# Grouped-query attention on one core: the one-block ScalarE tile of three-block jobs moves into the second bank of the transposes' tile

## The chip, the cores and the metric

The kernel runs on one core of one Trainium2 chip. The metric is the device time of the program in microseconds (us). A core has engines that run side by side, each in the order of its own program: TensorE (PE; its weight loads are listed as PEld), VectorE (DVE), ScalarE (ACT), GpSimd (POOL) and SyncE (SP, which issues transfers). They wait for each other through semaphores. Matmul results go to PSUM, eight banks of 512 float32 values on each of 128 partitions; everything else lies in SBUF.

## The reference

Attention with 32 query heads and 8 key/value heads, 8 batches, 512 positions, head size 64, all float32:

```python
batch, seq, n_heads, n_kv_heads, dim = 8, 512, 32, 8, 64
...
scores = np.einsum('bhqd,bhkd->bhqk', Q, K_expanded) * scale
weights = np.exp(scores - np.max(scores, axis=-1, keepdims=True))
weights = weights / (np.sum(weights, axis=-1, keepdims=True) + 1e-10)

output = np.einsum('bhqk,bhkd->bhqd', weights, V_expanded)
```

`K_expanded` and `V_expanded` repeat each key/value head for its four query heads; `scale` is 1/8.

## The kernel before

**Jobs and blocks.** One job is one key/value head of one batch with its four query heads: 64 jobs, `j` = 0 to 63. The four query heads are two pairs (`i` = 0, 1), the 512 keys four chunks of 128 (`kc`), and `m` is the head within a pair. A block is the scores of one head for one chunk of keys: 128 keys on the partitions, 512 queries in the free dimension, one PSUM bank. A job has 16 blocks. For every block the exponential of the scores is written to `pt` in fp16; the maximum is not subtracted. A second path for inputs outside its bounds, `general_path`, follows at the end and does not run for these inputs.

**Who takes the exponential.** ScalarE takes most blocks, two at a time: `act_tile(j, n)` makes the scores of its blocks in a tile `ps` of two banks (L199) and reads them with one ACTIVATE (L217). VectorE and GpSimd take the first two or three blocks of pair 1, with integer arithmetic: VectorE makes `u` from the scores (L228) and `f` from `u` (L249), GpSimd makes `g` and `w` from `f` (L241, L245), and VectorE adds `u` and `w` into `pt` (L262, in `exp_d4`, one job later). Three blocks are taken in the wide jobs, `WIDE(j)`: j = 10, 12, ..., 62, which is 27 jobs. ScalarE has 14 blocks in seven tiles of two in the other jobs. In a wide job it has 13: tiles 0 to 3 are pair 0, tile 4 is one single block (pair 1, chunk 1, `m` = 1, which stands in the second half of its tile), and tiles 5 and 6 are two blocks each.

**PSUM.** All eight banks are taken: `s_pool` has two score tiles of two banks, used in turn by `act_tile`; `d_pool` has one tile of two banks, used in turn by VectorE's score blocks and by the transposes of Q; `pv_pool` has one tile of two banks for the output sums. A tile that is asked for again is only written when its last readers are done.

**Order.** The order of every engine's work is written out by hand, in the loop over the jobs. While job `j` makes its scores, the product of weights and values (`pv`, L293) of job `j - 1` is cut into pieces that stand between the score tiles: pair 0 in two halves of 16 matmuls ahead of tile 2 and tile 3, pair 1 in pieces cut at `cut`, behind tiles 4, 5 and 6. For wide jobs `cut` is (4, 18): 4, 14 and 14 matmuls. `norm` divides by the sums (L336, L340) and frees the `pv` tile. Within `pv(j, 1)` the chunks of keys are taken in the order 2, 3, 1, 0, so the blocks that VectorE writes come last.

**Around the change.** Behind tile 3 the loop asks for a `d_ps` tile, `bank`. Into its first half `trans_q` writes the eight transposes of the queries of job `j + 2` (L164), as bf16, 1024 columns wide, which fills one bank. VectorE copies them to `qt` (L167). Then come `exp_d4` of the job before (L262), `exp_d2` of this job (L249, which sets GpSimd going), and tile 4. In odd jobs the second half of `bank` takes the third VectorE block of the wide job that follows. In wide jobs from 10 to 60 the second half stays unused; job 62 has no transposes.

Of the kernel before, what the change touches and what calls it, by code (L numbers as in the profile page):

```python
# [11 lines left out]
FP32 = mybir.dt.float32  # L12
# [46 lines left out]
def fast_path(ctx, tc, Q, K, V, out, flag):  # L59
    nc = tc.nc  # L60
    B, S, H, D = Q.shape
# [22 lines left out]
    s_pool = ctx.enter_context(tc.tile_pool(name="sps", bufs=2, space=PS))  # L84
# [15 lines left out]
    def load_k(b, lo=0, hi=KV):  # L100
        if b not in kn:
            kn[b] = knat_pool.tile([128, SC, KV, D], BF16, name="k_nat")
        nc.gpsimd.dma_start(  # L103
            out=kn[b][:, :, lo:hi, :],
            in_=K[b, :, lo:hi, :].rearrange("(sc p) g d -> p sc g d", p=128),
        )


    def load_v(b, lo=0, hi=KV, chunks=range(SC)):
        for sc in chunks:  # L110
            nc.gpsimd.dma_start(  # L111
                out=vt[b % 2][:, sc, lo:hi, 0:D],
                in_=V[b, sc * 128:(sc + 1) * 128, lo:hi, :],
            )
# [6 lines left out]
    def load_q(u, cuts=(0, 2 * HPG)):  # L121
        b, gp = divmod(u, GP)
        h0 = gp * 2 * HPG
        qn[u] = qnat_pool.tile([128, SC, 2 * HPG, D], BF16, name="q_nat")
        for lo, hi in zip(cuts[:-1], cuts[1:]):
            nc.gpsimd.dma_start(  # L126
                out=qn[u][:, :, lo:hi, :],
                in_=Q[b, :, h0 + lo:h0 + hi, :].rearrange("(sc p) h d -> p sc h d", p=128),
            )

    def d_tile():
        return d_pool.tile([128, 2, S], FP32, name="d_ps")
# [15 lines left out]
    def dma_k(b):  # L148
        kt[b] = kt_pool.tile([128, 2, GP, S], BF16, name="kt")
        for sc in range(SC):  # L150
            nc.sync.dma_start_transpose(
                out=kt[b][:, 0, :, sc * 128:(sc + 1) * 128],
                in_=kn[b][:, sc, :, :].rearrange("p g d -> p (g d)"),
            )
        for to, of in ((0, 64), (64, 0)):
            nc.sync.dma_start(out=kt[b][to:to + 64, 1, :, :], in_=kt[b][of:of + 64, 0, :, :])

    def trans_q(j, bank, lo=0, hi=NPAIR):
        u, g = divmod(j, 2)
        ps = bank.bitcast(BF16).rearrange("p (i sc c) -> p i sc c", i=NPAIR, sc=SC)  # L160
        for i in range(lo, hi):
            for sc in range(SC):
                h = g * HPG + 2 * i
                nc.tensor.transpose(ps[:, i, sc, :], qn[u][:, sc, h:h + 2, :], ident)  # L164
        if u not in qt:
            qt[u] = qt_pool.tile([128, 2, NPAIR, S], BF16, name="qt")
        return lambda: nc.vector.tensor_copy(  # L167
            out=qt[u][:, g, lo:hi, :], in_=ps[:, lo:hi, :, :].rearrange("p i sc c -> p i (sc c)")
        )

    def check_v(b, sc):
        n = b * SC + sc
        nc.vector.tensor_reduce(  # L173
            out=okv[:, n:n + 1], in_=vt[b % 2][:, sc, :, 0:D], op=ALU.max, axis=AX.XY,
            apply_absolute_value=True,
        )
# [6 lines left out]
    def taken(j):  # L183
        return 3 if WIDE(j) else 2

    def act_tiles(j):
        every = [(i, kc, m) for i in range(NPAIR) for kc in range(SC) for m in range(2)]
        first = DPAIR * SC * 2
        mine = [n for n in range(len(every)) if not first <= n < first + taken(j)]
        groups = [[n for n in mine if n // 2 == h] for h in range(len(every) // 2)]  # L190
        return [[every[n] for n in group] for group in groups if group]
# [3 lines left out]
    def scores(j, ps, i, kc, m):  # L195
        u, g = divmod(j, 2)
        b, gp = divmod(u, GP)
        keys = kt_first[:, gp, :, :] if b == 0 else kt[b][:, :, gp, :]
        nc.tensor.matmul(  # L199
            ps,  # L200
            keys[64 * m:64 * m + 64, g ^ m, kc * 128:(kc + 1) * 128],
            qt[u][64 * m:64 * m + 64, g, i, :],
            start=True,
            stop=True,
        )

    def open_job(j):
        pt = pt_pool.tile([128, NPAIR, SC, 2, S], FP16, name="pt")
        jobs.setdefault(j, {}).update(pt=pt, pv={})

    def act_tile(j, n):
        group = act_tiles(j)[n]
        i, kc, lo = group[0]
        ps = s_pool.tile([128, 2, S], FP32, name="s_ps")
        for _, _, m in group:
            scores(j, ps[:, m, :], i, kc, m)
        nc.scalar.activation(  # L217
            out=jobs[j]["pt"][:, i, kc, lo:, :], in_=ps[:, lo:, :], func=EXP, scale=scale
        )

    def exp_d(j, lo, hi, ps):
        st = jobs.setdefault(j, {})
        if "u" not in st:
            for name, dtype in (("u", I16), ("f", I16), ("g", BF16), ("w", BF16)):
                st[name] = dve_pool.tile([128, 3, S], dtype, name=name + "16")[:, 0:taken(j), :]
        for n in range(lo, hi):
            scores(j, ps[:, n - lo, :], DPAIR, n // 2, n % 2)
        return lambda: nc.vector.tensor_scalar(  # L228
            out=st["u"][:, lo:hi, :], in0=ps[:, 0:hi - lo, :], scalar1=A_U, scalar2=B_U,
            op0=ALU.mult, op1=ALU.add,  # L230
        )


    def by_pool(j):
        return 3 <= j < NJOB - 1
# [19 lines left out]
    def exp_d3(j, engine):  # L255
        st = jobs[j]
        correction(engine, st["f"], st["g"], st["w"])
# [144 lines left out]
    bank = d_tile()  # L402
# [4 lines left out]
    bank = d_tile()  # L407
# [3 lines left out]
    for j in range(NJOB):  # L411
        end = j == NJOB - 1
        last = j - 1
        late = last >= 0
        u, g = divmod(j, 2)
        b, gp = divmod(u, GP)
        open_job(j)
        if j == 1:

            nc.gpsimd.tensor_copy(out=gate, in_=jobs[0]["pt"][0:1, 0, SC - 1, 0, 0:1])  # L420
            load_q(2)
            load_q(3)
        if g == 0 and u >= 1 and u + 3 < NU:
            load_q(u + 3)
        if (gp, g) == (1, 0) and b + 1 < B:
            load_k(b + 1)
        if 3 <= 2 * gp + g < 3 + SC and b + 1 < B:
            load_v(b + 1, chunks=(2 * gp + g - 3,))
        if gp == 2 and g == 0 and b + 1 < B:
            dma_k(b + 1)  # L430

        cut = (4, 18) if taken(j) > 2 else (11, 19)
        act_tile(j, 0)
        if j == 0:
            trans_q(0, bank[:, 1, :], 1, NPAIR)()
            act_tile(j, 1)
            exp_d(j, 0, 2, d_tile())()
        else:
            exp_d(j, 0, 2, d_tile())()
            act_tile(j, 1)  # L440

        if j == 8:
            check_v(0, 0)
        if g == (b < B - 1) and j > 1:
            check_v(b, gp)
        if late:
            pv(last, 0, 0, 16)
        act_tile(j, 2)
        if late:
            pv(last, 0, 16, 32)  # L450
            norm(last, 0)
        act_tile(j, 3)

        reads = []
        if not end:
            bank = d_tile()

            ahead = (j + 1,) if j < 7 else (8, 9) if j == 7 else (j + 2,)
            for n, to in enumerate(ahead):
                if to < NJOB:  # L460
                    reads.append(trans_q(to, bank[:, n, :]))
            if j == 1:
                for swap in range(2):
                    reads.append(first_k(1, swap, bank[:, 1, swap * S // 2:]))
            elif j > 1 and b == 0 and gp + 1 < GP:
                reads.append(first_k(gp + 1, g, bank[:, 1, :]))
        else:
            pv(j, 0, 0, 16)
        for read in reads:
            read()  # L470

        if late and by_pool(last):
            exp_d4(last)
        check_sums()
        exp_d2(j)
        if not by_pool(j):
            exp_d3(j, nc.vector)
            exp_d4(j)
        act_tile(j, 4)
        if late:  # L480
            pv(last, 1, 0, cut[0])
        act_tile(j, 5)
        if not end and taken(j + 1) > 2:
            exp_d(j + 1, 2, taken(j + 1), bank[:, 1:2, :])()
        if late:
            pv(last, 1, *cut)
        act_tile(j, 6)
        if late:
            pv(last, 1, cut[1], 32)
            norm(last, 1)  # L490
            del jobs[last]
        if end:
            pv(j, 0, 16, 32)
            norm(j, 0)
            pv(j, 1, 0, 32)
            norm(j, 1)
# [118 lines left out]
```

## Time and profile before

| | |
|---|---|
| median time of three runs | 424.62 us (lowest 424.06) |
| span of the profiled execution, first to last instruction | 422.0 us |
| granted TensorE clock, mean | 0.984 |
| busy, share of the span: TensorE / VectorE / ScalarE / GpSimd | 91% / 82% / 96% / 69% |
| one ACTIVATE of two blocks (421) / of one block (27) | 1086 / 753 ns |
| scores, one matmul of 512 columns | 372 to 388 ns |

The profiled execution has no time of its own beside its span; 424.62 us is the median of executions that were timed. Durations of ScalarE's instructions overlap: a new one starts before the last has ended, so the step from one end to the next is shorter than a duration. Idle time is put down to the engine that ended it. Matmul durations overlap as well, and the two scores of a tile run side by side.

### The profile page before, as it was taken

To read this page: it belongs to the slowest core of one execution; us is meant where nothing else is said; L and a number is where in the kernel's file an instruction comes from. 1 tells how busy PE (TensorE), PEld (TensorE's weight loads), DVE (VectorE), ACT (ScalarE), POOL (GpSimd) and SP (SyncE) were. 2 spreads that over 40 slices of the span, in tenths; PEclk is the share of its full clock that TensorE was granted. 3 is DMA by queue.
4 is the path that set the end of the run, shared out by engine and by line. 5 is a ranking of instruction groups with operands and counts; after the bars stand their busy time and mean duration, and the time that the engine had idled before them with its cause. 6 is when DMAs were issued, how large, how long until landed. Compare 5 with 4: busy or idle time off the path is not lost.

```text
span 422.0 us, 13063 instructions
## 1 busy us (share of the span) xinstructions
PE 385.7 (91%) x5689; PEld 233.6 (55%) x5689; DVE 344.9 (82%) x611; ACT 404.2 (96%) x449; POOL 291.8 (69%) x209
## 2 busy tenths in 40 slices
PE   6889999999999999999999999999999999999983
PEld 2446565555555555555555555555555555555552
DVE  2697788889888888888888888888989888898875
ACT  3899999999999999999999999999999999999992
POOL 8504656778758876787866887677885887666560
PEclk9599999999999999999999999999999999999998
DMA  9996986599967998499964999649996799642223
GB/s 97 177 139 159 217 165 151 70 207 187 191 151 99 216 198 160 133 198 133 229 150 116 206 163 255 157 69 200 157 225 155 122 206 207 148 123 101 102 91 115
DMA packets 91438, 66.95 MB, mean 159 GB/s; under 512 B 52080, under 2 KB 74608, under 8 KB 91376
## 3 DMA queue, kind: packets, MB, share of 16 engines
q0 software_dynamic: 56544, 25.17, 51.1%
q1 hardware_dynamic: 34832, 40.90, 34.5%
q8 instruction: 45, 0.74, 0.7%
q14 instruction: 17, 0.14, 0.1%
HBM read 50.33 MB, written 33.55 MB: 199 GB/s over the span
## 4 chain that ended last, share of the span: by engine, by line
ACT 54%; PE 36%; DVE 6%; issue 1%; POOL 1%; ACTq 0%; DVEq 0%; POOLq 0%
ACT pt L217 54%; PE s_ps L199 17%; PE pv L293 16%; PE d_ps L199 1%; DVE o_sb L340 1%; PE d_ps L164 1%; DVE pt L262 1%; DVE u L228 1%; DVE qt L167 1%; DVE w L245 0%; POOL q_nat L126 0%; DVE kt_first L146 0%; ACTq L217 0%; PE d_ps L143 0%; DVE f L249 0%
## 5 line engine op out<-in xcount | busy, mean ns | idle before, releaser
L217 ACT ACTIVATE pt<-s_ps 128x1024 f16<-128x1024 f32 (+1 forms) x448 | 402.9, 1066 | 9.1 <-PE s_ps L199 9.0
L293 PEld LDWEIGHTS <-pt 128*128 128x128 f16 x4096 | 144.2, 98 | 86.8 <-issue 50.4
L293 PE MATMUL pv<-v,pt 128*128 128x65 bf16 x4032 | 183.2, 195 | 2.6 <-DVE o_sb L340 1.6
L199 PE MATMUL s_ps<-qt,kt 64*128 64x512 bf16 x757 | 152.7, 384 | 19.9 <-ACT pt L217 15.4
L245 POOL TENSOR_TENSOR w<-g,f 128x1024 bf16<-128x1024 bf16 (+1 forms) x60 | 153.7, 2562 | 5.0
L241 POOL TENSOR_SCALAR g<-f 128x1024 bf16<-128x1024 int16 (+1 forms) x60 | 73.9, 1231 | 110.1 <-DVE f L249 110.1
L228 DVE TENSOR_SCALAR u<-d_ps 128x1024 int16<-128x1024 f32 (+1 forms) x91 | 96.2, 1058 | 1.1 <-PE d_ps L199 1.1
L340 DVE TENSOR_TENSOR o_sb<-pv,inv 128x512 f32<-128x512 f32 x125 | 86.5, 692 | 4.5 <-DVE inv L336 0.2
L199 PEld LDWEIGHTS <-kt 64*128 64x128 bf16 x896 | 49.0, 93 | 62.6 <-issue 35.0
L336 DVE RECIPROCAL inv<-pv 128x8 f32<-128x8 f32 x125 | 25.9, 207 | 55.8 <-PE pv L293 55.4
L262 DVE TENSOR_TENSOR pt<-u,w 128x1536 uint16<-128x1536 int16 (+1 forms) x64 | 50.9, 795 | 0.2
L167 DVE COPY qt<-d_ps 128x1024 bf16<-128x1024 bf16 (+1 forms) x65 | 44.3, 683 | 4.5 <-PE d_ps L164 2.9
L164 PE MATMUL d_ps<-ident,q_nat 128*128 128x128 bf16 x512 | 40.1, 222 | 1.1 <-DVE kt_first L146 0.9
L164 PEld LDWEIGHTS <-q_nat 128*128 128x128 bf16 x512 | 29.2, 98 | 15.8 <-issue 15.7
L199 PE MATMUL d_ps<-qt,kt 64*128 64x512 bf16 x139 | 31.4, 376 | 0.3
L249 DVE TENSOR_SCALAR f<-u 128x1536 int16<-128x1536 int16 (+1 forms) x64 | 30.8, 481 | 0.0
L111 POOL DMA_DIRECT2D v<-in_V_dram x32 | 29.0, 910 | 0.4 <-issue 0.4
L126 POOL DMA_DIRECT2D q_nat<-in_Q_dram x34 | 27.4, 806 | 1.5 <-DMA q_nat<-in_Q_dram 1.3
L199 PE MATMUL s_ps<-qt,kt_first 64*128 64x512 bf16 x112 | 23.7, 419 | 4.1 <-ACT pt L217 3.0
L173 DVE TENSOR_REDUCE okv<-v 128x1 f32<-128x512 bf16 x32 | 21.6, 675 | 0.0
L199 PEld LDWEIGHTS <-kt_first 64*128 64x128 bf16 x128 | 8.0, 95 | 12.2 <-issue 8.4
L103 POOL DMA_DIRECT2D k_nat<-in_K_dram x10 | 7.7, 770 | 1.0 <-POOLq L599 0.8
(40 smaller groups left out, 37.6 us busy)
## 6 DMA issues: line engine op xcount, KB each, us to landing
out_dram<-o_sb SPq DMA_DIRECT2D x31, 1024.0 KB, 6.9
q_nat<-in_Q_dram POOLq DMA_DIRECT2D x31, 512.0 KB, 6.3
k_nat<-in_K_dram POOLq DMA_DIRECT2D x7, 512.0 KB, 8.6
v<-in_V_dram POOLq DMA_DIRECT2D x28, 128.0 KB, 7.6
kt<-kt SPq DMA_DIRECT2D x14, 256.0 KB, 4.6
out_dram<-o_sb SPq DMA_DIRECT2D x4, 256.0 KB, 2.4
kt<-k_nat SPq DMA_TRANSPOSE x28, 5.6
v<-in_V_dram POOLq DMA_DIRECT2D x4, 96.0 KB, 7.8
```

Source lines behind the costliest of these rows:

```text
L111: nc.gpsimd.dma_start(out=vt[b % 2][:, sc, lo:hi, 0:D], in_=V[b, sc * 128:(sc + 1) * 128, lo:hi, :],)
L164: nc.tensor.transpose(ps[:, i, sc, :], qn[u][:, sc, h:h + 2, :], ident)
L167: return lambda: nc.vector.tensor_copy(out=qt[u][:, g, lo:hi, :], in_=ps[:, lo:hi, :, :].rearrange("p i sc c -> p i (sc c)"))
L199: nc.tensor.matmul(ps, keys[64 * m:64 * m + 64, g ^ m, kc * 128:(kc + 1) * 128], qt[u][64 * m:64 * m + 64, g, i, :], start=True, stop=True,)
L217: nc.scalar.activation(out=jobs[j]["pt"][:, i, kc, lo:, :], in_=ps[:, lo:, :], func=EXP, scale=scale)
L228: return lambda: nc.vector.tensor_scalar(out=st["u"][:, lo:hi, :], in0=ps[:, 0:hi - lo, :], scalar1=A_U, scalar2=B_U, op0=ALU.mult, op1=AL ...
L241: engine.tensor_scalar(out=g, in0=f, scalar1=-EXP_F1, scalar2=EXP_K * 2.0 ** (24 * as_bits), op0=ALU.add, op1=ALU.mult,)
L245: engine.tensor_tensor(out=w, in0=g, in1=f.bitcast(FP16) if as_bits else f, op=ALU.mult)
L249: nc.vector.tensor_single_scalar(out=st["f"], in_=st["u"], scalar=1023, op=ALU.bitwise_and)
L262: nc.vector.tensor_tensor(out=st["pt"][:, DPAIR, :, :, :].rearrange("p kc m q -> p (kc m) q")[:, 0:n, :].bitcast(U16), in0=st["u"], in1=st ...
L293: nc.tensor.matmul(st["pv"][i][:, m, qc, :], st["pt"][:, i, kc, m, qc * 128:(qc + 1) * 128], vt[b % 2][:, kc, 2 * gp + g, :], start=(n < 2 ...
L340: nc.vector.tensor_tensor(out=osb[u][:, :, h:h + 2, :].rearrange("p qc m d -> p m qc d"), in0=sums[:, :, :, 0:D], in1=inv[:, :, :, None].t ...
```

## The change

In wide jobs tile 4 no longer takes a score tile. It gets the `d_ps` tile `bank`, as soon as this has been asked for, and its one score matmul goes to the second half of it. With it, the matmul and the ACTIVATE move in the program from behind the transposes, their copy, `exp_d4` and `exp_d2` to directly behind tile 3. Other jobs are as before.

```diff
-    def act_tile(j, n):
+    def act_tile(j, n, spare=None):
         group = act_tiles(j)[n]
         i, kc, lo = group[0]
-        ps = s_pool.tile([128, 2, S], FP32, name="s_ps")
+        ps = s_pool.tile([128, 2, S], FP32, name="s_ps") if spare is None else spare
         for _, _, m in group:
             scores(j, ps[:, m, :], i, kc, m)
         nc.scalar.activation(
...
         if not end:
             bank = d_tile()
+            if taken(j) > 2:
+                act_tile(j, 4, bank)
 
             ahead = (j + 1,) if j < 7 else (8, 9) if j == 7 else (j + 2,)
...
             exp_d3(j, nc.vector)
             exp_d4(j)
-        act_tile(j, 4)
+        if taken(j) == 2:
+            act_tile(j, 4)
         if late:
             pv(last, 1, 0, cut[0])
         act_tile(j, 5)
```

## The prediction

> **What bounds the kernel now.** I read the page's table of busy times first, then the chain that ended last, then the groups of ScalarE by shape.
>
> ```profile
> PE 385.7 (91%) x5689; PEld 233.6 (55%) x5689; DVE 344.9 (82%) x611; ACT 404.2 (96%) x449; POOL 291.8 (69%) x209
> ...
> ACT 54%; PE 36%; DVE 6%; issue 1%; POOL 1%; ACTq 0%; DVEq 0%; POOLq 0%
> ```
>
> ```profile
> L217 ACT ACTIVATE pt<-s_ps 128x1024 f16<-128x1024 f32 x421 | 390.0, 1086 | 9.1 <-PE s_ps L199 9.0
> L217 ACT ACTIVATE pt<-s_ps 128x512 f16<-128x512 f32 x27 | 20.3, 753 | 0.0
> ```
>
> ScalarE (ACT) works for 96% of the span; of its 9.1 us of waiting 6.2 are the first tile's. So every microsecond by which ScalarE gets its next scores too late lengthens the kernel. The 27 instructions of 512 columns are the one-block tiles that the change touches (jobs 10, 12, ..., 62). TensorE (PE) has 91%: it can run ahead of ScalarE only as far as score tiles come free, and has little time to catch up.
>
> Then I read one wide job on TensorE in the timeline (start, length, engine), job 30.
>
> ```profile
> 203.37 0.39 PE L199 MATMUL s_ps<-qt,kt 64*128 64x512 bf16 x2
> 203.69 0.62 PE L164 MATMUL d_ps<-ident,q_nat 128*128 128x128 bf16 x8
> 204.28 0.37 PE L199 MATMUL s_ps<-qt,kt 64*128 64x512 bf16 x1
> 204.58 0.30 PE L293 MATMUL pv<-v,pt 128*128 128x65 bf16 x4
> 205.19 0.39 PE L199 MATMUL s_ps<-qt,kt 64*128 64x512 bf16 x2 [0.31 <-ACT pt L217]
> 205.52 0.61 PE L293 MATMUL pv<-v,pt 128*128 128x65 bf16 x14
> 206.06 0.39 PE L199 MATMUL s_ps<-qt,kt 64*128 64x512 bf16 x2
> ```
>
> In order: scores of tile 3, eight transposes, the single score of tile 4, four PV matmuls, the scores of tile 5 (which waited 0.31 us for ScalarE to free tile 3's buffer), 14 PV, tile 6. ScalarE's one-block tile, from the answer for its line in this stretch:
>
> ```profile
> L217 ACT ACTIVATE pt<-s_ps x1: 752/752/752, 204.9 to 204.9; 128x512 f16<-128x512 f32 x1
> ```
>
> It starts at 204.88 and ends at 205.63; tile 3 ends at 205.14, tile 5 starts at 205.62.
>
> **What the change removes.** Tile 4 no longer takes one of the two score buffers, so tile 5's scores no longer wait for tile 3. What that wait costs ScalarE is seen in the ends of its instructions: a full tile ends 0.917 us after the one before, tile 5 ends 1.011 us after tile 4. So 0.094 us per wide job, 27 x 0.094 = 2.5 us, is all that can be won here (0.6%).
>
> **What it moves and adds.** One weight load, one score matmul and, with it, one ACTIVATE move ahead of eight transposes. Nothing is passed on the other queues. The price of the matmul is unchanged (0.37 us, 0.22 to the next start). But the built order of the changed kernel shows a new wait: the first of the eight transposes waits for the ACTIVATE that reads tile 4's scores, in jobs 10 to 60, all that have transposes; job 62 has none. The two lie in different halves of one d_ps tile, and the transposes' write is ordered behind the read of the other half. In the kernel before they waited only for VectorE's `u`, long done (202.79).
>
> Behind the waiting transpose, in TensorE's order, are the other seven, four PV matmuls and the scores of tile 5, which ScalarE needs directly after tile 4. So ScalarE stands idle for the whole of that row:
>
> - ScalarE's end of tile 4 to the first transpose: 0.051 us (as 205.143 to 205.194, tile 3's end to tile 5's scores).
> - First transpose to the first PV start: 0.401 us to the last transpose's start, plus 0.18 (last transpose to the next matmul of another kind, 204.097 to 204.277): 0.58. Transposes followed by PV are not in the trace; the bounds are 0.056 (one transpose's step) and 0.305 (score start to PV start, 204.28 to 204.58) for the 0.18. I take the row with transposes in it.
> - Four PV matmuls to the next score: 0.103 to the last start plus 0.128 (203.246 to 203.373): 0.231.
> - Score start to ACTIVATE start: 0.428 (205.194 to 205.622).
>
> Together 1.29 us after tile 4's end, at 206.93 instead of 205.62: **1.30 us later**. After a wait a full ACTIVATE takes 1.02 us, as tile 5's did before, so ends move as starts do. Nothing hides this: TensorE gives matmuls in order, and ScalarE has no other scores. From there TensorE repeats its old pace (tile 6's scores 0.86 us later, within ScalarE's step), so the loss isn't won back.
>
> **What is late next.** VectorE copies the transposes 0.04 us after their end: at 206.34 instead of 204.35, 1.99 us later, which is 0.69 more than the shift. Behind it in VectorE's order stand L262 (0.68) and L249 (0.55). L262's result is needed by the last eight PV matmuls of the job, about 0.2 us after it is there: no cost. L249's `f` starts POOL: `g` and `w` of the wide job (1.47 and 3.10 us) come 0.69 us late, and the next job's L262 needs `w`:
>
> ```profile
> 207.76 3.10 POOL L245 TENSOR_TENSOR w<-g,f 128x1536 bf16<-128x1536 bf16 x1
> ...
> 211.10 0.95 DVE L262 TENSOR_TENSOR pt<-u,w 128x1536 uint16<-128x1536 int16 x1
> ...
> 211.80 0.45 PEld L293 LDWEIGHTS <-pt 128*128 128x128 f16 x8 [0.42 <-issue]
> 212.30 0.10 PEld L199 LDWEIGHTS <-kt 64*128 64x128 bf16 x2
> ```
>
> `w` ends at 210.86, L262 starts at 211.10. The shortest distance in the trace is 0.035 us, so 0.21 is spare and L262 starts 0.69 - 0.21 = 0.47 us late. The PV matmuls in front of the odd job's tile 6 already wait for it (eight take 0.45 of loads where 0.30 would do), so these scores come 0.47 late. ScalarE has 0.23 in hand there (scores at 212.305 plus 0.428 plus 1.02 is 213.75; tile 6 ends at 213.98). So 0.25 us more per pair; its bounds are 0 (POOL's delay absorbed) and 0.47 (nothing in hand).
>
> **Sum.** 26 x (1.30 + 0.25) = 40.3 us; job 62 wins 0.1. From the profiled span of 422.0 that gives 462 us; the median, 424.62, lies 2.6 above the span, so the time to expect is **465 us**, slower by 9.5%. With the bounds of the two open terms: 26 x (1.18 + 0) = 31 to 26 x (1.43 + 0.47) = 49 us, that is 455 to 474.
>
> **Rule and row, first place.** The row is a write behind a read of the other half of one tile. The Trainium skill, page "PSUM — Partial Sum Buffer", section "Summary: rules for kernel authors", says that PSUM may be read while a matmul runs if the matmul targets a different bank, guarded by bank. By that the transposes need not wait, and the sum would be the gain of 2.5 us (first rival); the trace of before has no such pair in one tile to test it, and it is the order of the built program that keeps the wait.
>
> **Rivals.**
>
> A. *The wait costs nothing or is not there.* Place: the first transpose. If it were released before TensorE reaches it (at about 203.9), or the transposes ran beside the ACTIVATE, only the won 2.5 us would remain: 422 us, not slower. It decides below 8.5 / 26 = 0.33 us of ScalarE idling per pair. For it: the halves are separate. Against: the wait is in the program, and its releaser ends at 205.63, 1.7 us after TensorE arrives. Chance 0.04.
>
> B. *The clock falls.* Stretches with TensorE's busy time and the granted clock:
>
> ```profile
> 5.62:9.03 3.41, 1.93 (x22) 1.00 1.36 138
> 9.03:19.27 10.24, 8.80 (x63) 0.50 1.57 167
> 22.69:26.10 3.41, 2.20 (x34) 1.00 1.24 207
> ```
>
> After 3.41 us with 57% busy the clock was halved for 10.24 us; after one with 64% it was not. The changed kernel leaves TensorE idle from about 203.97 to 205.68, 1.71 us, so a stretch of 3.41 us that holds it all is at most 50% busy. If the share in a fixed grid of 3.41 us decides, the point is 1.2 to 1.5 us of idling in one stretch; with 1.5, (3.41 - 1.71 + 2 x 0.21) / 3.41 = 0.62 of the 26 pairs hit it, 16. In the slow stretch a tile's scores and 16 PV took 1.54 us (16.16 to 17.70) against ScalarE's 0.92: 0.62 lost on each of 6.6 tiles in 10.24 us, 4.1 us, of which the wait itself may take in up to 1.7. So 16 x 2.4 to 4.1, 38 to 66 us more, about 517 us. Against: one single instance, at the start, where the 2.2 us before the warm-up were mostly empty as well. Chance 0.17.
>
> The Trainium skill, page "TensorE: Matmul & The Clock Gate", section "What's actually happening", has the clock fall after at least one idle window of about 3.4 us. By that no pair would hit it and the sum stays; the trace does not agree in full, since its stretch of 57% was followed by the half clock.
>
> C. *The first step alone*, with POOL's delay absorbed: 458 us. It lies inside the forecast's bounds and has its chance.
>
> **How the numbers follow.** Forecast 0.76 (455 to 474), rival A 0.04, rival B 0.17, anything else slower 0.03. Leaving out A and all of B would lose more than 0.2, so the range reaches into B: 453 to 505. About 2%, 8.5 us, can be told from no change here: faster 0.01, same 0.03, slower 0.96.
>
> **What would show it.** Right: TensorE's wait for the one-block ACTIVATE ahead of the transposes, about 1.6 us x 26; ScalarE's idle time ahead of tile 5 about 26 x 1.3 us, its busy time unchanged at 404; the odd job's tile 6 waiting by a few tenths. Wrong: if those waits are absent (A), if the granted clock drops between 80 and 400 us (B), or if ScalarE's idle time stands ahead of another tile, which would mean that TensorE doesn't keep its old pace behind the stall.

## The result

The changed kernel takes 471.72 us (median of 4 runs, 470.75 to 473.62) against 424.34 us (median of 4) for the kernel before, so 47 us more: 1.113 times as long, 95% interval 1.110 to 1.116. One of the four executions of before, at 455.51 us, was in a slow state and is left out of the ratio; the other three have a median of 424.06. The forecast was 465 us, with a range of 453 to 505. The profiled execution spans 472.0 us, 50.0 more than the 422.0 of before.

### The profile after

The same lines of the page, and the clock row of its second part (40 slices of the span, in tenths):

```profile
PE 393.9 (83%) x5689; PEld 239.9 (51%) x5689; DVE 348.5 (74%) x611; ACT 408.6 (87%) x449; POOL 292.0 (62%) x209
...
PEclk8899999999899898999999898998999988999899
...
PE 32%; ACT 32%; DVE 19%; POOL 14%; issue 2%; ACTq 0%; DVEq 0%; POOLq 0%
```

All shares have fallen while the counts of instructions are the same: nothing got more work, everything waits longer. TensorE's busy time is 8 us longer, under the lower clock. The chain that ended last has changed its nature. ScalarE was 54% of it, now 32%; VectorE went from 6 to 19% and GpSimd from 1 to 14%. And the clock row has 8s in the middle, where the page of before has 9s from the third slice to the last but one:

```profile
PEclk9599999999999999999999999999999999999998
```

ScalarE by shape (busy, mean ns of one, then idle time ahead of the group and who ended it):

```profile
L217 ACT ACTIVATE pt<-s_ps 128x1024 f16<-128x1024 f32 x421 | 394.3, 1056 | 54.6 <-PE s_ps L199 54.1
L217 ACT ACTIVATE pt<-d_ps 128x512 f16<-128x512 f32 x27 | 18.1, 669 | 0.0
```

The busy times hardly differ from before, the idle time went from 9.1 to 54.6 us. One pair of jobs, 32 and 33, on TensorE (start, length; the rows between the odd job's parts are left out):

```profile
239.44 0.61 PE L164 MATMUL d_ps<-ident,q_nat 128*128 128x128 bf16 x8 [1.62 <-ACT pt L217]
239.88 0.29 PE L293 MATMUL pv<-v,pt 128*128 128x65 bf16 x4
240.10 0.39 PE L199 MATMUL s_ps<-qt,kt 64*128 64x512 bf16 x2
240.42 0.60 PE L293 MATMUL pv<-v,pt 128*128 128x65 bf16 x14
240.96 0.39 PE L199 MATMUL s_ps<-qt,kt 64*128 64x512 bf16 x2
...
246.71 0.33 PE L293 MATMUL pv<-v,pt 128*128 128x65 bf16 x5
247.70 0.27 PE L293 MATMUL pv<-v,pt 128*128 128x65 bf16 x3 [0.67 <-DVE pt L262]
247.90 0.39 PE L199 MATMUL s_ps<-qt,kt 64*128 64x512 bf16 x2
```

The same stretch on ScalarE:

```profile
238.75 0.64 ACT L217 ACTIVATE pt<-d_ps 128x512 f16<-128x512 f32 x1
240.53 7.44 ACT L217 ACTIVATE pt<-s_ps 128x1024 f16<-128x1024 f32 x8 [1.15 <-PE s_ps L199]
248.33 1.02 ACT L217 ACTIVATE pt<-s_ps 128x1024 f16<-128x1024 f32 x1 [0.36 <-PE s_ps L199]
```

TensorE's transposes wait 1.62 us here for the one-block ACTIVATE (1.42 to 1.71 over the 26 times, 41.7 us in all), tile 5 stalls ScalarE for 1.15 us, and tile 6 of the odd job for 0.36 us. Two stalls per pair, at the two places that were named. The chain of this stretch, in order of time, shows how they hang together (start, length, what; steps of 0.1 us and less are left out):

```profile
235.13 4.27 ACT pt L217 x5
...
239.44 0.62 PE d_ps L164 x8
...
240.15 0.69 DVE qt L167
240.84 0.60 DVE pt L262
241.44 0.48 DVE f L249
...
242.01 1.47 POOL g L241
...
243.55 3.11 POOL w L245
...
246.68 0.96 DVE pt L262
```

The chain leaves ScalarE at the end of tile 4 and does not come back over tile 5. It goes through the transposes, the copy, L262, `f`, GpSimd's `g` and `w`, and the next L262, on which the PV matmuls at 247.70 wait.

To compare runs I use the steps from one end of a ScalarE instruction to the next, taken from the traces. A full tile's step is 0.917 us when nothing is late. Over a pair of jobs:

| run | tile 5, wide | tile 6, wide | tile 0, odd | tile 6, odd | pair, us | time, us |
|---|---|---|---|---|---|---|
| before | 1.01 | 0.92 | 0.92 | 0.92 | 12.50 | 424 |
| changed | 2.17 | 0.92 | 0.92 | 1.38 | 14.12 | 471.7 |
| copy last | 2.17 | 0.91 | 0.92 | 0.92 | 13.66 | 454.4 |
| filled wait | 2.17 | 0.91 | 0.92 | 1.38 | 14.12 | 465.4 |
| tile 5 first | 0.92 | 1.68 | 1.37 | 1.42 | 14.12 | 465.4 |
| no PV in between | 2.05 | 0.99 | 0.94 | 1.41 | 14.12 | 472.4 |
| tile 5 first, copy last | 0.92 | 1.68 | 0.92 | 0.92 | 13.17 | 445.9 |
| order alone | 1.08 | 0.92 | 0.92 | 1.31 | 12.96 | 435.5 |
| score behind the transposes | 0.92 | 0.92 | 1.40 | 1.42 | 13.39 | 446.4 |
| two tiles, not changed | 1.01 | 0.92 | 0.92 | 0.92 | 12.50 | 421.3 |
| two tiles, changed | 0.92 | 0.92 | 0.92 | 0.92 | 12.41 | 419.7 |
| two tiles, changed, copy last | 0.92 | 0.92 | 0.92 | 0.92 | 12.41 | 418.8 |

The values are medians over the pairs; of the changed kernel and the run with no PV in between, the pair is that of the pairs at the full clock. The steps that are not listed do not differ from before, so what the four listed ones lose adds up to what the pair loses.

The 26 pairs account for the whole difference: 26 x (14.12 - 12.50) = 42.1 us, and 8.0 us more in 12 pairs that were longer than 14.12 (14.5 to 15.0), together 50.1 of the 50.0 us.

### The profile page after: what moved, and what is told of

It is laid out like the page before. It is cut to its first block, busy times and chain, and to the rows that moved or that the text cites. A ratio compares the mean times of both kernels' runs of the same rounds, so it can differ in the third digit from the quotient of the medians.

```text
span 472.0 us, 13035 instructions
## 1 busy us (share of the span) xinstructions
PE 393.9 (83%) x5689; PEld 239.9 (51%) x5689; DVE 348.5 (74%) x611; ACT 408.6 (87%) x449; POOL 292.0 (62%) x209
## 4 chain that ended last, share of the span: by engine, by line
PE 32%; ACT 32%; DVE 19%; POOL 14%; issue 2%; ACTq 0%; DVEq 0%; POOLq 0%
ACT pt L217 32%; PE pv L293 14%; PE s_ps L199 11%; POOL w L245 9%; DVE pt L262 6%; PE d_ps L164 6%; POOL g L241 4%; DVE qt L167 3%; DVE o_sb L340 3%; DVE f L249 2%; DVE u L228 1%; PE d_ps L199 1%; DVE inv L336 1%; DVE ok L304 1%; DVE w L245 0%
## 5 line engine op out<-in xcount | busy, mean ns | idle before, releaser
L217 ACT ACTIVATE pt<-s_ps 128x1024 f16<-128x1024 f32 x421 | 394.3, 1056 | 54.6 <-PE s_ps L199 54.1
L293 PE MATMUL pv<-v,pt 128*128 128x65 bf16 x4032 | 191.6, 199 | 15.7 <-DVE pt L262 9.8
L293 PEld LDWEIGHTS <-pt 128*128 128x128 f16 x4096 | 153.0, 101 | 101.1 <-issue 53.9
L199 PE MATMUL s_ps<-qt,kt 64*128 64x512 bf16 x730 | 149.0, 403 | 6.2 <-ACT pt L217 3.3
L164 PE MATMUL d_ps<-ident,q_nat 128*128 128x128 bf16 x512 | 41.6, 227 | 42.8 <-ACT pt L217 41.7
L199 PEld LDWEIGHTS <-kt 64*128 64x128 bf16 x896 | 44.4, 94 | 45.6 <-issue 20.4
L164 PEld LDWEIGHTS <-q_nat 128*128 128x128 bf16 x512 | 32.5, 101 | 62.1 <-issue 62.0
L262 DVE TENSOR_TENSOR pt<-u,w 128x1536 uint16<-128x1536 int16 (+1 forms) x64 | 51.0, 797 | 8.1 <-POOL w L245 7.9
L199 PE MATMUL d_ps<-qt,kt 64*128 64x512 bf16 x166 | 43.2, 394 | 0.3
L249 DVE TENSOR_SCALAR f<-u 128x1536 int16<-128x1536 int16 (+1 forms) x64 | 30.8, 481 | 0.0
L217 ACT ACTIVATE pt<-d_ps 128x512 f16<-128x512 f32 x27 | 18.1, 669 | 0.0
```

What stands on the lines that cost most here:

```text
L199: nc.tensor.matmul(ps, keys[64 * m:64 * m + 64, g ^ m, kc * 128:(kc + 1) * 128], qt[u][64 * m:64 * m + 64, g, i, :], start=True, stop=True,)
L217: nc.scalar.activation(out=jobs[j]["pt"][:, i, kc, lo:, :], in_=ps[:, lo:, :], func=EXP, scale=scale)
L249: nc.vector.tensor_single_scalar(out=st["f"], in_=st["u"], scalar=1023, op=ALU.bitwise_and)
L262: nc.vector.tensor_tensor(out=st["pt"][:, DPAIR, :, :, :].rearrange("p kc m q -> p (kc m) q")[:, 0:n, :].bitcast(U16), in0=st["u"], in1=st ...
L293: nc.tensor.matmul(st["pv"][i][:, m, qc, :], st["pt"][:, i, kc, m, qc * 128:(qc + 1) * 128], vt[b % 2][:, kc, 2 * gp + g, :], start=(n < 2 ...
```

## Experiments

### What sets the length of a pair

The losses of tile 5 (1.16) and of the odd tile 6 (0.46) might be two costs that add up, or one chain might set the pair while the other stall lies beside it. Three edits tell these apart.

**VectorE's copy behind L262 and L249 in wide jobs.**

```diff
+        wide = taken(j) > 2
-        for read in reads:
+        for read in reads if not wide else []:
             read()
         if late and by_pool(last):
             exp_d4(last)
         check_sums()
         exp_d2(j)
+        for read in reads if wide else []:
+            read()
```

> The changed kernel, but in wide jobs VectorE does L262 and L249 ahead of the copy of the transposes, so that `f`, and with it GpSimd's `g` and `w`, no longer wait behind the one-block ACTIVATE. If the odd job's loss of 0.46 us at tile 6 comes from the late `w`, it goes: 26 x 0.46 = 12 us less, about 460 us, with tile 5 still ending 2.17 us after tile 4. If that loss is TensorE's own lack of lead behind the stall, nothing changes: 472 us.

Measured: 454.42 us, ratio 1.0705 (1.0668 to 1.0741). The odd tile 6 is on time in every pair, and tile 5 still ends 2.17 us after tile 4. The waits of GpSimd's result by VectorE, 7.9 us in the changed kernel, are no longer among VectorE's waits. So the odd job's stall comes from the late `w`, not from a lack of lead on TensorE. The pair is 1.155 us longer than before, tile 5's loss alone: 26 x 1.155 = 30.0 us over 424. That is 6 us less than I expected, since the clock fell only once in the 26 pairs (below).

**Tile 5's scores ahead of the transposes.**

```diff
             if taken(j) > 2:
                 act_tile(j, 4, bank)
+                act_tile(j, 5)
...
-        act_tile(j, 5)
+        if taken(j) == 2:
+            act_tile(j, 5)
```

> The changed kernel with tile 5's scores also ahead of the transposes in wide jobs; the wait itself stays. Tile 5 then ends 0.92 us after tile 4, and tile 6's scores, behind the transposes and 18 PV matmuls, come about 0.7 us too late. First theory (the late scores and the late `w` add up): per pair 0.70 + 0.46 in place of 1.16 + 0.46, 12 us less, and 8 less as TensorE idles under 1 us at a stretch: about 452 us. Second theory (the chain transposes, copy, L262, `f`, `g`, `w`, next L262, tile 6 alone sets the pair, 2.04 - 0.44 = 1.60 us, and the stall of tile 5 lies beside it): the odd job's loss grows to 0.9, only the clock's 8 us go, about 464 us.

Measured: 465.43 us, ratio 1.0980 (1.0960 to 1.0999). Tile 5 is on time, and the pair is as long as in the changed kernel, to 0.01 us: 14.12. The stall has only moved, to tile 6 and into the odd job, whose tiles 0 and 6 lose 0.45 and 0.50 us. VectorE's waits of this run (total, times, longest):

```profile
DVE qt L167 <- PE d_ps L164: 51.5, 30, 2.0
...
DVE pt L262 <- POOL w L245: 14.7, 26, 0.6
```

L262 waits for `w` in all 26 pairs. The second theory holds: the chain over the copy and GpSimd sets the pair. The 6 us that this run is faster are the clock's: it is not halved in any of the 26 pairs.

**No PV matmuls between the transposes and tile 5's scores.**

```diff
-        cut = (4, 18) if taken(j) > 2 else (11, 19)
+        cut = (0, 18) if taken(j) > 2 else (11, 19)
```

> The changed kernel with no PV matmuls between the transposes and tile 5's scores in wide jobs (0, 18 and 14 instead of 4, 14 and 14). Tile 5 ends about 0.22 us earlier. First theory (losses add up): 26 x 0.22 = 5.7 us less, about 466 us. Second theory (the chain over the copy and GpSimd sets the pair): the 0.22 us come back as a longer wait of the odd job's tile 6 (0.68 instead of 0.46), 472 us.

Measured: 472.43 us, ratio 1.1125 (1.1087 to 1.1164), the same as the changed kernel. Tile 5 comes 0.12 us earlier (0.22 had been expected: the step from the last transpose to a score takes 0.15 us, that to a PV matmul 0.06), and the pair stays at 14.12. What is won at tile 5 is lost again at the three tiles that follow in the table, 0.08, 0.02 and 0.03 us, and not at the odd tile 6 alone as expected. Taking work out of the stall that is seen first buys nothing.

**Both: tile 5 first and the copy last.**

> The changed kernel with both edits: tile 5's scores ahead of the transposes, and the copy behind L262 and L249. The chain over GpSimd is freed and the stall of tile 5 is gone, so what is left is tile 6, behind the transposes and 18 PV matmuls: it ended 1.68 us after tile 5 in the run with tile 5 first, 0.77 more than a step, less the 0.09 won at tile 5. 26 x 0.68 = 18 us over before, about 442 us. If the two losses were independent of each other this pair of edits would give 471.7 - 17 (copy last) - 6 (tile 5 first) = 449 us.

Measured: 445.88 us (four executions, 441.86 to 451.03). The ratio, 1.0497 (1.0435 to 1.0559), is that of three of them, whose median is 443.61; the one of 451.03 us has the lowest clock of the four, 0.958. The pair is 13.17, which is 0.67 over before, as worked out from tile 6's 1.68. In the profiled run, 443.61, two pairs have 14.60 where the clock fell; the executions differ in how often it did (mean granted clock 0.992 in the fastest, 0.969 in one of 448 us). The expected 442 is the time without such falls. The median lies between the two forecasts and can't tell them apart; the pair's length does, and it is the one that the chain gives (0.68 expected).

### The clock

In the changed kernel the granted clock was halved 12 times between 80 and 445 us, each time for 3.41 us. Two stretches of 3.41 us, each followed by the next (length, TensorE's busy time and matmuls, clock; the last two numbers are the DMA's):

```profile
121.89:125.30 3.41, 1.79 (x31) 1.00 0.64 85
125.30:128.71 3.41, 3.41 (x37) 0.50 0.43 73
108.23:111.64 3.41, 1.87 (x31) 1.00 0.83 105
111.64:115.05 3.41, 3.31 (x58) 1.00 1.15 186
```

In that run every stretch of the grid with 1.61 us or more of idling was followed by a half clock, and none with 1.54 or less. The waits are 1.42 to 1.71 us long, so a stretch has to hold all, or all but 0.1 us, of one of the longer ones; 12 do. The point is not the same in every run. With no PV in between, a stretch with 1.52 us of idling was followed by a half clock and one with 1.60 was not; with tile 5 first and the copy last, two of eleven stretches with 1.31 us were; at the start of the kernel before, one with 1.48 was. So the idling alone, as the trace gives it, is not the exact measure, and that stays open.

**The wait filled with matmuls.** Four matmuls of 512 columns, on zeros, into the score tile that tile 5 takes next.

```diff
                 act_tile(j, 4, bank)
+                if j < NJOB - 2:
+                    nxt = s_pool.tile([128, 2, S], FP32, name="s_ps")
+                    for n in range(NFILL):
+                        nc.tensor.matmul(nxt[:, n % 2, :], warm[:, 0:128], warm, start=True, stop=True)
...
-        act_tile(j, 5)
+        act_tile(j, 5, nxt if taken(j) > 2 and j < NJOB - 2 else None)
```

> The changed kernel with four more matmuls of 512 columns in the wait, written into the score tile that tile 5 overwrites afterwards; they add nothing to the result. They end before the one-block ACTIVATE does, so the wait keeps its length and TensorE is idle for under 0.6 us at a stretch instead of 1.6. If idling within one stretch of 3.41 us is what halves the clock, the clock is full from 80 to 450 us and the 8 us that the 12 longer pairs hold go: about 464 us. If the clock falls for another reason, or costs nothing, 472 us.

Measured: 465.43 us, ratio 1.0981 (1.0958 to 1.1004). The clock over 313 us, and that of the changed kernel over 363:

```profile
82.00:395.00 313.00, 280.30 (x3998) 1.00 0.86 153
```

```profile
82.00:445.00 363.00, 305.18 (x4436) 0.95 0.78 143
```

All 26 pairs are 14.11 to 14.13. More work on TensorE makes the kernel 6 us faster, since it is done where TensorE would have been idle. That the halved clock comes from the idling is shown by this run; its price is 6 us in the medians, 8 in the two profiled executions.

### Where the wait comes from

**The order alone.** Tile 4's score ahead of the transposes, but in a score tile.

```diff
-                act_tile(j, 4, bank)
+                act_tile(j, 4)
```

> The changed order alone: tile 4's score stands ahead of the transposes but goes to a score tile as before, so it waits for tile 2's ACTIVATE (204.23 in the old timeline) and the transposes start at about 204.5 instead of 203.7. Tile 5 is not late. The copy comes 0.8 us late, of which 0.44 are spare on the chain over GpSimd: 26 x 0.37 = 10 us, about 434 us. If the false wait were all and the copy's place nothing, 424 us; if the order were the cause of the loss, 472 us.

Measured: 435.46 us, ratio 1.0271 (1.0252 to 1.0290). Of the loss, 0.46 per pair (0.37 expected), 0.40 stand at the odd tile 6 and 0.07 at tile 5. VectorE waits for `w` in 26 pairs here too (13.4 us). The transposes and their copy come 0.89 us late in the trace (0.8 expected), which less the 0.44 spare is 0.45. So this delay, without any wait for the other half of a tile, costs nearly 12 us, by these waits over the copy.

**The score behind the transposes, in the same tile.**

```diff
-            if taken(j) > 2:
-                act_tile(j, 4, bank)
...
+        if not end and taken(j) > 2:
+            act_tile(j, 4, bank)
         for read in reads:
             read()
```

> The changed kernel with tile 4's score in the same second half, but behind the eight transposes and ahead of their copy. TensorE has its old order and waits for nothing new; in the built order it is now VectorE's copy, a second reader of the tile, that waits for the one-block ACTIVATE. It ends at 205.63 in the old timeline, so the copy comes at about 205.70 instead of 204.35, 1.34 us late, of which 0.44 are spare on the chain over GpSimd: 26 x 0.90 = 23 us, about 447 us, with tile 5 ending 0.92 us after tile 4 and all of the loss at the odd job's tile 6. If only TensorE's wait mattered, it would be 422 us.

Measured: 446.40 us, ratio 1.0537 (1.0511 to 1.0563). Waits of this run:

```profile
PE pv L293 <- DVE pt L262: 32.8, 53, 0.7
...
DVE qt L167 <- ACT pt L217: 29.2, 26, 1.2
DVE pt L262 <- POOL w L245: 14.7, 26, 0.6
```

TensorE's transposes are not held here, and ScalarE has tile 5 on time. The copy waits 26 times for ScalarE, which only reads the other half of the tile, and the pair is 0.89 longer, as expected from the chain. But half of that loss stands at another place than I expected: 0.49 us at tile 0 of the odd job and 0.50 at its tile 6 (less 0.10 won at tile 5). Ahead of the odd tile 0, the last eight PV matmuls of the wide job wait for VectorE's L262, which stands behind the late copy; the same stall shows with tile 5 first.

**Two tiles of one bank each in place of one of two.** VectorE's `u` of two blocks becomes two instructions. First without the change, then with it:

```diff
     def d_tile():
-        return d_pool.tile([128, 2, S], FP32, name="d_ps")
+        return [d_pool.tile([128, S], FP32, name=f"d_ps{n}") for n in range(2)]
...
+        def read():
+            for n in range(lo, hi):
+                nc.vector.tensor_scalar(out=st["u"][:, n, :], in0=ps[n - lo], ...
...
-                act_tile(j, 4, bank)
+                act_tile(j, 4, bank[1])
```

The last line stands in the second kernel alone; in the last job, the sums of pair 0 take a new tile of two banks in the same place.

> The kernel before, with two tiles of one bank each in place of the `d_ps` tile of two banks; VectorE's `u` of two blocks becomes two instructions of 512 columns (2 x 0.69 us in place of 1.21, about 0.1 us more per job on VectorE). It is the base for the next run. VectorE has that time ahead of its reciprocals, so the time should stay within 1% of 424 us, tile 5 ending 1.01 us after tile 4 as before.

> The same two tiles of one bank, with the change: tile 4's score goes to the second of them ahead of the transposes, which go to the first. If the wait follows the tile and not the bank, the transposes do not wait for the ACTIVATE, the whole loss of 47 us is gone, and tile 5 ends 0.92 us after tile 4: 27 x 0.09 = 2.5 us below the run with two tiles and no change, about 422 us. If the loss came from the place of the score matmul ahead of the transposes, or from ScalarE's reading beside TensorE's writing in neighbouring banks, a good part of the 47 us stays.

Measured: 421.34 us, ratio 0.9941 (0.9925 to 0.9957), without the change, and 419.72 us, ratio 0.9886 (0.9866 to 0.9907), with it. In the built order the transposes then have no wait for ScalarE, and none shows in the trace (first line below; the other two are from one wide job; L165 and L218 are L164 and L217 of the kernel before):

```profile
L165 PE MATMUL d_ps<-ident,q_nat 128*128 128x128 bf16 x512 | 40.1, 222 | 0.2 <-DVE kt_first L147 0.2
...
201.66 0.62 PE L165 MATMUL d_ps<-ident,q_nat 128*128 128x128 bf16 x8
...
202.65 0.67 ACT L218 ACTIVATE pt<-d_ps 128x512 f16<-128x512 f32 x1
```

With the change tile 5 ends 0.92 us after tile 4, in place of 1.01, and most pairs take 12.41 us, in place of 12.50. Between the two medians that makes 1.6 us, where 2.5 had been expected; six pairs are about 0.1 us longer than the others. So the same score in a bank of its own, at the same place in the order, loses none of the 47 us. Cause and price belong to the shared tile. When ScalarE comes to read tile 4, behind tile 3, the transposes have been over for 0.2 to 0.4 us. In the changed kernel, too, they could have been done before that read: TensorE stood ready from 237.82 us, the eight take 0.61, and the read began at 238.75. So what happens when ScalarE reads one of these two banks while TensorE writes the other is not tested by any run here. The 2.4 us of the run without the change do not come from the pairs (12.50 as before) but from ahead of job 10: job 9's last tile ends at 74.05 us in place of 76.46. In the profiles of the kernels with one `d_ps` tile that end lies between 76.0 and 77.3 us, in the three with two tiles between 73.5 and 74.9; what shortens the start is open.

**The same with the copy last in wide jobs.**

> The run with two one-bank tiles and the change, with VectorE's copy behind L262 and L249 in wide jobs, so that GpSimd's `w` comes earlier. There some six pairs were 0.1 us longer than the others, at the odd job's tile 6. If that is the chain over GpSimd, they fall back to 12.41 us: 0.6 us less, about 419 us. If not, the same time as without this edit, 419.7.

Measured: 418.76 us, ratio 0.9888 (0.9868 to 0.9907). All 26 pairs are 12.41 now; the six of 12.48 to 12.52 in the run above were the chain over GpSimd again. 12.41 is 13 steps of 0.917 and one of 0.49, ScalarE without a gap (of its 6.4 us of idle time 5.6 are the first tile's):

```profile
L218 ACT ACTIVATE pt<-s_ps 128x1024 f16<-128x1024 f32 x421 | 398.2, 1281 | 6.4 <-PE s_ps L200 6.4
```

Against the run before it, 0.9886, the ratio shows no gain; only the pairs show the 0.6 us. These two are the fastest kernels of this study, 1.1% ahead of the kernel before, which is less than the 2% that the prediction took as the least that can be told.

## Why the prediction was right, and where not

- **The bound and the wait: right.** ScalarE bounds the kernel; the transposes wait for the one-block ACTIVATE in 26 jobs, 1.60 us each on the mean (forecast about 1.6), and ScalarE's busy time is nearly unchanged (404.2 and 408.6 us). Rival A, that the wait costs nothing, fell.
- **The first term, 1.30 us, was too large: 1.16.** The mis-sized part is the step from the last transpose to the first PV matmul, taken as 0.18 between bounds of 0.056 and 0.305. In the trace after, the PV matmuls start 0.444 us after the first transpose instead of 0.58. The last transpose starts 0.388 us after the first, so the step is 0.056, the lower bound itself. The 0.18 belonged to a step from a transpose to a score, of another kind than the one wanted.
- **The second term, 0.25 us, was too small: 0.46.** The lateness of `w` is measured against the shift of ScalarE. With a shift of 1.16 in place of 1.30 the copy is later against it by 0.14 more, and by a further 0.05 since it starts 0.105 us after the end of the transposes, not 0.04; `f` follows it. What was spare (0.21 on VectorE, 0.23 on ScalarE) held.
- **The sum, 1.55 per pair, came out at 1.62, for a reason that the prediction did not name.** I added a stall and a second stall behind it. The runs with tile 5 first and with no PV in between show that the sum is one chain: the copy, and `f` with it, is 2.04 us late against ScalarE's end of tile 4 as compared with before, less 0.44 spare, 1.60. The prediction's own numbers held this chain: 1.99 us late less 0.44 is its 1.55, whatever the first term is. So the error of the first term cancelled in the second, and that the total came out well is no sign that the two terms were right. Had I taken the first term for the cost and tried to shorten it, as the run with no PV in between does, I would have forecast a gain that is not there. Rival C, the first step alone at 458 us, is the case that the run with the copy last makes: 454.4, with 1.16 in place of 1.30.
- **The clock: a rival with 0.17, not in the sum; it came, smaller.** Its condition was right in kind: a stretch of a fixed grid that holds the whole wait. Forecast were 16 pairs and 10.24 us each, as at the start of the trace of before; there were 12, and 3.41 us each. So 8 us in place of 38 to 66. In the profiled run the point lay between 1.54 and 1.61 us of idling, above the 1.2 to 1.5 that I had read from two early stretches; in other runs it did not. By the prediction's own list a clock that drops between 80 and 400 us was a sign of being wrong, and it dropped. The forecast of 465 is the time without that, which the run with the filled wait gives (465.4). That 471.7 still lies within 455 to 474 is in part luck, because these bounds came from the other two terms. In the profiled executions, 1.6 x 26 = 42 us of chain plus 8 of clock are the measured 50.
- **The two rules.** The Trainium skill's page "PSUM — Partial Sum Buffer", section "Summary: rules for kernel authors", which lets a matmul write while another bank is read, is not tested by the run with two tiles, where the transposes end before ScalarE's read of the other bank begins. What the run shows is that the wait came from the shared tile in the program: without it the same order has no wait. A read beside a write shows only for banks of different tiles, where ScalarE reads a score tile while the transposes are written (before, from 203.69 us on) and keeps its step of 0.917 us, as the rule allows. The Trainium skill's page "TensorE: Matmul & The Clock Gate", section "What's actually happening", asks for an idle window of about 3.4 us before the clock falls; here it fell behind a window that was 52% busy (1.79 of 3.41 us), and the measurement decides.

## What to carry to other kernels

An unused bank inside a tile is not free: readers and writers of the two halves were ordered against each other here as if they touched the same data, TensorE behind ScalarE and even VectorE's read behind ScalarE's. A tile of its own for each bank removed that. When an instruction is made to wait, follow every engine that it feeds to where the next loss is, and ask which chain is the longest; the two stalls of the bounding engine in this loop body were not costs that add up, and shortening the one that the profile shows first may buy nothing. A wait of TensorE also cost clock behind it here, and work put into the wait was cheaper than idling.

## What the runs showed that was not expected

- In the profiled run of the changed kernel the clock fell to half behind single stretches of 3.41 us with 1.61 us or more of idling, and came back after one stretch of 3.41 us, in the middle of the kernel. At the start it falls once for 10.24 us in the trace of before and twice for 3.41 us in that of the changed kernel.
- Whether it falls seems to depend on how the pair fits the grid, as far as two profiled runs tell. With the copy last the pair takes 13.657 us, almost exactly four stretches (13.653). The wait keeps its place against the grid, cut in two, and the clock fell once in 26 pairs; with the same wait and 14.12 us per pair it fell 12 times.
- Under the half clock a pair of the changed kernel lost 0.4 to 0.9 us. The loss of tile 6 in the odd job, 0.46, then all but vanishes (its step is 0.92 to 0.96): part of the price is hidden behind the chain over GpSimd. Where the odd tile 6 is on time, a pair lost more: 1.28 us with the copy last and 1.43 with tile 5 first and the copy last.
